# Attention scores as three products of high and low parts in place of one fp32 product

## The chip, the cores and the metric

The kernel runs on one core of one Trainium2 chip. The metric is the device time of one execution in microseconds, the median of the runs shown. Five engines work side by side, each through its own list of instructions in a fixed order: TensorE (PE: matmuls; PEld: the loads of their stationary operand), VectorE (DVE), ScalarE (ACT), GpSimd (POOL) and SyncE (SP, which here only issues transfers).

## The reference

One encoder layer over 1024 rows of 1024 numbers, in fp32. What the change touches is the first part: two attentions over the same normalised rows.

```python
# differential attention, 8 heads, two maps of width 64 each
s = einsum('bqhd,bkhd->bhqk', qq, kk) * scale + bias        # bias: -slope * distance
p = softmax(where(allowed, s, -inf))                        # allowed: key chunk <= query chunk
a = p(map 1) - lam * p(map 2);   o = a @ v                  # then a norm over each head
# chunk attention, 8 heads of width 64: each chunk of 64 sees itself and 8 chunks before it
s = einsum('bcqhd,bckhd->bhcqk', qc, kb) * dh**-0.5 + bias;  o = softmax(s) @ vb
```

Then `h = x + W_out(gates * projections)`, and a retrieval layer (PEER): each row picks 8 x 16 of 16384 experts by two top-16 searches, takes the experts' `u` rows, a gelu, a softmax weight, and sums their `v` rows.

## The kernel before

The rows are 8 blocks of 128. Blocks 0 and 1 form the first group, blocks 2 to 7 the second. The stages, in the order of the program:

- `Dense` (lines 236 to 302) multiplies the normalised rows by `w_in`, tile by tile, and stores q, k, v and gates to DRAM. Its products use three single-pass matmuls of high and low parts: `split` (L124) casts fp32 to the type fp32r on ScalarE (L126: the high part) and subtracts on VectorE (L127: the low part), `mm3` (L129) issues high x high, high x low, low x high.
- `attention` (L304) runs four times: for block 0, for block 1, for blocks 2 and 3 (below: the pair stage), and for blocks 4 to 7 (below: the rest stage). `weave` (L52) alternates its steps with those of other generators: the pair stage with `Dense` of the second group, the rest stage with `merge` and `sel` of blocks 2 and 3.
- In an attention, `kv_load` fetches keys, values and queries of one head from DRAM into tiles with two buffers each. Partitions 0 to 63 of a key tile hold one map (or one of two heads), 64 to 127 the other. `softmax_in` issues the score products (L347) of the two halves, a piece of up to 512 keys at a time; VectorE adds the bias, writes to SBUF and keeps the minimum (L353); ScalarE takes the exponential (L360). A score tile is one of three PSUM buffers. `later` transposes (L203) and multiplies by the values (L372).
- `merge`/`mop` (L478, L849), `sel` (L857: the choice of experts, `top16` at L558 to L563 and `choose`), `gates` (L643) and, at the end, `dense_experts` (L681), which streams all experts for blocks 2 to 5. For blocks 0, 1, 6 and 7 `experts` (L790) gathers the chosen rows: 128 `u` and 128 `v` rows per block and token, each a gather by GpSimd (L804) and one VectorE product over 128x1024 (L810 for `u`, L816 for `v`). These gather products are spread over the whole program: those of blocks 0 and 1 run beside the attentions.

The generators give an order of issue; a scheduler behind them then fixes the order of each engine's list by its own estimate of when operands are ready. So an edit in one place moves instructions of all stages.

Of the kernel before, what the change touches and what calls it, by code (L numbers as in the profile page):

```python
# [7 lines left out]
F32 = mybir.dt.float32  # L8
F32R = mybir.dt.float32r
# [6 lines left out]
P = 128  # L16
# [56 lines left out]
def layer_kernel(ctx, tc, x, w1, w_in, b_gate, lq1, lk1, lq2, lk2, subln, rel,  # L73
# [230 lines left out]
    def attention(wk, LM, gi, blocks, tr, need, put_d, put_c):  # L304
# [4 lines left out]
        t0 = (blocks[0] - GROUPS[gi][0]) * P  # L309

        def kv_load(ksrc, vsrc, qsrc, kb0):
            kt = wk.tile([P, LM], F32, name="kt", tag="kt")
            vt = wk.tile([P, LM // P, P], F32, name="vt", tag="vt")
            qt = wk.tile([P, T], F32, name="qt", tag="qt")
            for g2 in range(gi + 1):
                ob = GROUPS[g2][0]
                s0 = max(kb0, ob)
                e0 = min(blocks[-1] + 1, ob + len(GROUPS[g2]))
                if s0 >= e0:
                    continue  # L320
                nc.sync.dma_start(kt[:, (s0 - kb0) * P:(e0 - kb0) * P], ksrc[g2][:, (s0 - ob) * P:(e0 - ob) * P])
                nc.sync.dma_start(vt[:, s0 - kb0:e0 - kb0, :],
                                  vsrc[g2][(s0 - ob) * P:(e0 - ob) * P, :].rearrange("(n p) f -> p n f", p=P))
            nc.sync.dma_start(qt, qsrc[:, t0:t0 + T])
            return kt, vt, qt

        def sc_tile():
            return psp.tile([P, 512], F32, name="sc", tag="sc", bufs=3)
# [9 lines left out]
        def softmax_in(todo):  # L338


            mns = [None] * len(todo)
            for n in range(len(todo[0][2])):
                os = []
                for q, k, pieces, pt, scale in todo:
                    k0, k1, bias = pieces[n]
                    o = sc_tile()
                    nc.tensor.matmul(o[:, :k1 - k0], q, k[:, k0:k1], start=True, stop=True)  # L347
                    os.append(o)
                for i, (q, k, pieces, pt, scale) in enumerate(todo):
                    k0, k1, bias = pieces[n]  # L350
                    d = k0 - pieces[0][0]
                    mn = sm.tile([P, 1], F32, name="mn", tag="mn", bufs=8)
                    nc.vector.tensor_tensor_reduce(pt[:, d:d + k1 - k0], os[i][:, :k1 - k0], bias, scale,  # L353
                                                   3.0e38 if mns[i] is None else mns[i], OP.add, OP.min, mn)
                    mns[i] = mn
            zs = []
            for i, (q, k, pieces, pt, scale) in enumerate(todo):
                d = pieces[-1][1] - pieces[0][0]
                z = sm.tile([P, 1], F32, name="z", tag="z", bufs=8)
                nc.scalar.activation(pt[:, :d], pt[:, :d], AF.Exp, bias=mns[i], scale=-1.0, accum_out=z)  # L360
                zs.append(z)
            return zs
# [12 lines left out]
        def diff_a(h, i, qb):  # L375
            if i == 0:
                need(h)
                kv[h] = kv_load({g: kd[g][h] for g in kd}, {g: vd[g][h] for g in vd}, qd[gi][h], 0)
            kt, vt, qt = kv[h]
            n = (qb + 1) * P  # L380
            pieces = [(c, min(n, c + 512), dm[:, 896 - P * qb + c:896 - P * qb + min(n, c + 512)])
                      for c in range(0, n, 512)]
            pm = [wk.tile([P, LM], F32, name=f"p{m}", tag="p", bufs=PBUFS) for m in range(2)]
            Z = softmax_in([(qt[rs, i * P:(i + 1) * P], kt[rs], pieces, pt, 2.0 ** -(h + 1))
                            for rs, pt in zip(HALVES, pm)])
            rz1 = sm.tile([P, 1], F32, name="rz1", tag="rz1")
            rz2 = sm.tile([P, 1], F32, name="rz2", tag="rz2")
            f = sm.tile([P, 1], F32, name="f", tag="f")
            nc.vector.reciprocal(rz2, Z[1])
            nc.vector.reciprocal(rz1, Z[0])  # L390
            nc.vector.scalar_tensor_tensor(f, Z[0], nlam, rz2, op0=OP.mult, op1=OP.mult)
            nc.vector.scalar_tensor_tensor(pm[0][:, :n], pm[1][:, :n], f, pm[0][:, :n], op0=OP.mult, op1=OP.add)

            if i % tr == 0:
                ohs[h] = wk.tile([P, tr, P], F32, name="oh", tag="oh")
            oh = ohs[h]

            def later():
                o = pv(pm[0], qb + 1, vt, 0)
                oi = oh[:, i % tr, :]  # L400
                nc.scalar.activation(oi, o[:, :P], AF.Copy, scale=rz1)
                k = h * nb + i
                nc.scalar.activation(scr, oi, AF.Square, accum_out=ssh[:, k:k + 1])
                if i % tr == tr - 1:
                    put_d(h, i + 1 - tr, transposes([oh[:, i2, :] for i2 in range(tr)])[:, :tr * P])
            return later
# [14 lines left out]
        def chunk_a(hp, i, qb):  # L421
            kb0 = max(0, blocks[0] - 4)
            if i == 0:
                need(8 + hp)
                kv[8 + hp] = kv_load({g: kc[g][hp] for g in kc}, {g: vc[g][hp] for g in vc}, qc[gi][hp], kb0)
            if i % tr == 0:
                och[hp] = wk.tile([P, tr, P], F32, name="och", tag="oh")
            oh = och[hp]
            kt, vt, qt = kv[8 + hp]
            k0 = max(0, qb - 4)  # L430
            j0 = (k0 - qb + 4) * P
            off = (k0 - kb0) * P - j0
            pts = [wk.tile([P, LM], F32, name=f"pc{m}", tag="p", bufs=PBUFS) for m in range(2)]
            todo = []
            for m in range(2):
                pieces = []
                if j0 < 384:
                    pieces.append((off + j0, off + 384, far[:, j0:384]))
                c = max(j0, 384)
                pieces.append((off + c, off + 640, nbias[:, 2 * hp + m, c - 384:256]))  # L440
                todo.append((qt[HALVES[m], i * P:(i + 1) * P], kt[HALVES[m]], pieces, pts[m], 1.0))
            rzs = []
            for z in softmax_in(todo):
                rz = sm.tile([P, 1], F32, name="rz", tag="rzc", bufs=8)
                nc.vector.reciprocal(rz, z)
                rzs.append(rz)

            def later():
                for rs, pt, rz in zip(HALVES, pts, rzs):
                    o = pv(pt, qb + 1 - k0, vt, k0 - kb0)  # L450
                    nc.scalar.activation(oh[:, i % tr, rs], o[:, rs], AF.Copy, scale=rz)
                if i % tr == tr - 1:
                    put_c(hp, i + 1 - tr, transposes([oh[:, i2, :] for i2 in range(tr)])[:, :tr * P])
            return later
# [498 lines left out]
```

## Time and profile before

| | us |
|---|---|
| median of 3 runs (lowest, highest) | 3437.65 (3435.08, 3438.16) |
| the profiled execution | 3433.26 |
| its span, first to last instruction | 3431.5 |
| PE busy in the span | 3085.0 (90%) |
| DVE busy | 2700.0 (79%) |
| ACT busy | 1446.3 (42%) |
| POOL busy | 1249.1 (36%) |

The stages lie in the span about so: attention of blocks 0 and 1 from 0 to 300 us, the pair stage from 450 to 960, the rest stage from 1000 to 1460, merges, gates and choices up to 1960, the streamed experts from 2020 to the end. A busy share is an average over stages; what an edit is worth is read from the stage that it is in. PE counts as busy while any matmul is in flight, drain included.

### The profile page before, as it was taken

The numbers are of one execution on the slowest core, as the hardware profiler recorded it, in microseconds if no ns is written. First come the engines' busy times: TensorE is split into PE (matmuls) and PEld (weight loads), VectorE is DVE, ScalarE is ACT, GpSimd is POOL, SyncE is SP. The second block draws the span as 40 slices with busy tenths as digits, with TensorE's granted clock in tenths as the row PEclk, the third lists the DMA queues.
The fourth block names the chain that finished last, engine by engine and source line by source line (L and its number), as shares of the span: only waits on it lengthen the run. The fifth ranks groups of instructions, "written<-read, shape, count | busy, mean of one in ns | idle before, by whom it ended". The sixth has DMA issues, their size and how long they took to land.

```text
span 3431.5 us, 48288 instructions
## 1 busy us (share of the span) xinstructions
PE 3085.0 (90%) x16032; PEld 2551.8 (74%) x16032; DVE 2700.0 (79%) x5848; ACT 1446.3 (42%) x3029; POOL 1249.1 (36%) x1028
## 2 busy tenths in 40 slices
PE   7987699999979886987798359999999999999998
PEld 7986578888857654676677348888888888888886
DVE  4436897777779899987976978889998888999543
ACT  5634433434423544567669523333233333333332
POOL 0000455555544522344000144555555555555000
PEclk9999899999989987998898669999999999999999
DMA  7675999999999975898544499999999999999531
GB/s 240 219 244 189 374 333 348 333 352 334 326 340 351 324 236 186 281 360 331 203 162 157 145 343 319 346 350 339 347 345 345 346 342 344 346 340 349 166 123 49
DMA packets 406122, 987.13 MB, mean 288 GB/s; under 512 B 43184, under 2 KB 188400, under 8 KB 403696
## 3 DMA queue, kind: packets, MB, share of 16 engines
q0 software_dynamic: 147456, 536.94, 44.1%
q1 hardware_dynamic: 258416, 447.11, 37.4%
q8 instruction: 126, 2.06, 0.2%
q14 instruction: 124, 1.02, 0.1%
HBM read 905.72 MB, written 78.15 MB: 287 GB/s over the span
## 4 chain that ended last, share of the span: by engine, by line
PE 71%; issue 12%; DVE 7%; DMA 7%; ACT 2%; POOL 1%; SPq 0%; DVEq 0%; POOLq 0%; ACTq 0%
PE ph L134 20%; PE mm L134 16%; PE acc L710 15%; PE acc L717 5%; PE mm L490 5%; PE sc L347 3%; PE pv L372 3%; PE tr L203 2%; DMA ge<-in_u_dram,ei 2%; DVE junk L810 1%; DVE p L353 1%; POOL ge L804 1%; DMA rb<-rst 1%; DMA ge<-in_v_dram,ei 1%; DVE acc L816 1%
## 5 line engine op out<-in xcount | busy, mean ns | idle before, releaser
L804 POOL DMA_INDIRECT ge<-in_u_dram,ei x512 | 619.1, 1209 | 1249.0 <-DVE junk L810 396.4
L804 POOL DMA_INDIRECT ge<-in_v_dram,ei x512 | 629.8, 1230 | 683.2 <-DVE acc L816 462.0
L816 DVE SCALAR_TENSOR_TENSOR acc<-ge,a,acc 128x1024 f32<-128x1024 f32 x512 | 655.1, 1280 | 26.2 <-DMA ge<-in_v_dram,ei 20.1
L810 DVE SCALAR_TENSOR_TENSOR junk<-ge,xs 128x1024 bf16<-128x1024 f32 x512 | 624.7, 1220 | 53.7 <-DMA ge<-in_u_dram,ei 45.7
L127 DVE TENSOR_TENSOR wl<-wr,wh 128x1024 fp32r<-128x1024 f32 x232 | 283.6, 1223 | 233.1 <-ACT wh L126 107.5
L126 ACT CAST wh<-wr 128x1024 fp32r<-128x1024 f32 x232 | 243.7, 1051 | 406.5 <-PE ph L134 267.1
L134 PE MATMUL ph<-x2h,wh 128*128 128x512 f32 x1024 | 400.3, 391 | 11.8 <-ACT wh L126 10.4
L134 PE MATMUL ph<-x2l,wh 128*128 128x512 f32 x1024 | 399.9, 390 | 0.0
L134 PE MATMUL mm<-xh,wh 128*128 128x256 f32 (+1 forms) x1248 | 372.0, 325 | 0.7 <-ACT st L286 0.5
L134 PE MATMUL mm<-xl,wh 128*128 128x256 f32 (+1 forms) x1248 | 366.8, 321 | 1.4 <-DVE xl L232 1.3
L134 PEld LDWEIGHTS mm<-xh,wh 128*128 128x128 f32 x1248 | 236.9, 190 | 24.8 <-ACT st L286 2.3
L134 PE MATMUL ph<-x2h,wl 128*128 128x512 f32 x1024 | 253.1, 389 | 0.0
L134 PEld LDWEIGHTS mm<-xl,wh 128*128 128x128 f32 x1248 | 236.4, 190 | 21.5 <-DVE xl L232 2.1
L126 ACT CAST vh<-vr 128x512 fp32r<-128x512 f32 x256 | 140.4, 619 | 264.8 <-PE acc L717 243.4
L134 PE MATMUL mm<-xh,wl 128*128 128x256 f32 (+1 forms) x1248 | 234.4, 323 | 0.0
L134 PEld LDWEIGHTS ph<-x2h,wh 128*128 128x128 f32 x1024 | 193.2, 189 | 52.9 <-ACT wh L126 10.8
L134 PEld LDWEIGHTS ph<-x2l,wh 128*128 128x128 f32 x1024 | 193.2, 189 | 40.2
L134 PEld LDWEIGHTS ph<-x2h,wl 128*128 128x128 f32 x1024 | 192.3, 188 | 40.0
L347 PE MATMUL sc<-kt,qt 64*128 64x256 f32 (+3 forms) x608 | 202.1, 533 | 17.8 <-DVE mn L353 10.2
L710 PE MATMUL acc<-vh,ah 128*128 128x512 f32 x768 | 198.3, 389 | 0.0
L126 ACT CAST ah<-ge 128x512 fp32r<-128x512 f32 x128 | 79.7, 622 | 281.4 <-DVE ge L757 266.3
L134 PEld LDWEIGHTS mm<-xh,wl 128*128 128x128 f32 x1248 | 184.7, 189 | 16.8
(199 smaller groups left out, 5741.6 us busy)
## 6 DMA issues: line engine op xcount, KB each, us to landing
vr<-in_v_dram SPq DMA_DIRECT2D x128, 512.0 KB
wr<-in_ut_dram SPq DMA_DIRECT2D x128, 512.0 KB
wr<-in_w_in_dram SPq DMA_DIRECT2D x104, 512.0 KB
gdr<-gst SPq DMA_DIRECT2D x16, 2048.0 KB
gj<-gdr SPq DMA_DIRECT2D x512, 64.0 KB
wr<-in_w_bd_dram SPq DMA_DIRECT2D x40, 512.0 KB
wr<-in_w_out_dram SPq DMA_DIRECT2D x40, 512.0 KB
wr<-in_wq_dram SPq DMA_DIRECT2D x40, 512.0 KB
```

The source lines that it names most:

```text
L126: nc.scalar.copy(hi, raw)
L127: nc.vector.tensor_sub(lo, raw, hi.bitcast(F32))
L134: nc.tensor.matmul(o, w[a][:, k, :], xx[b][:, k, :], start=(i == 0), stop=(i == last))
L203: nc.tensor.transpose(o[:, i * P:(i + 1) * P], s, ident)
L347: nc.tensor.matmul(o[:, :k1 - k0], q, k[:, k0:k1], start=True, stop=True)
L372: nc.tensor.matmul(o[:, :P], aT[:, j - c, :], vt[:, v0 + j, :], start=(j == 0), stop=(j == n - 1))
L490: nc.tensor.matmul(o, w[:, k, :], xx[:, k, :], start=(k == 0), stop=(k == K - 1))
L710: nc.tensor.matmul(acc[i][hf], a[x][:, i * P:(i + 1) * P], b[y][:, hf * 512:hf * 512 + 512], **kw)
L717: nc.tensor.matmul(o, aa[:, 3 * P:4 * P], bb[:, cs], start=(n == 0), stop=(n == len(todo) - 1))
L804: nc.gpsimd.indirect_dma_start(out=t, out_offset=None, in_=src, in_offset=bass.IndirectOffsetOnAxis(ap=ei[:, k:k + 1], axis=0))
L810: nc.vector.scalar_tensor_tensor(junk, t, 1.0, xs, op0=OP.mult, op1=OP.mult, accum_out=hid[:, k:k + 1])
L816: nc.vector.scalar_tensor_tensor(acc, t, a[:, k:k + 1], acc, op0=OP.mult, op1=OP.add)
```

## The change

Keys and queries are loaded into tiles of type fp32r and split there: ScalarE casts the loaded tile into a new tile (`kth`, `qth`: the high part), VectorE subtracts in place (`ktl`, `qtl` then hold the low part). Each score product, one fp32 matmul before, becomes three fp32r matmuls that accumulate in PSUM: high x high, high query x low key, low query x high key. The loop is turned round so that the two halves alternate within each of the three.

```diff
         def kv_load(ksrc, vsrc, qsrc, kb0):
-            kt = wk.tile([P, LM], F32, name="kt", tag="kt")
+            ktl = wk.tile([P, LM], F32R, name="ktl", tag="ktl")
+            kt = ktl.bitcast(F32)
             vt = wk.tile([P, LM // P, P], F32, name="vt", tag="vt")
-            qt = wk.tile([P, T], F32, name="qt", tag="qt")
+            qtl = wk.tile([P, T], F32R, name="qtl", tag="qtl")
+            qt = qtl.bitcast(F32)
...
             nc.sync.dma_start(qt, qsrc[:, t0:t0 + T])
-            return kt, vt, qt
+            n = (blocks[-1] + 1 - kb0) * P
+            two = []
+            for lo, m, name in ((ktl, n, "kt"), (qtl, T, "qt")):
+                hi = wk.tile(list(lo.shape), F32R, name=name + "h", tag=name + "h")
+                split(lo[:, :m].bitcast(F32), hi[:, :m], lo[:, :m])
+                two.append((hi, lo))
+            return two[0], vt, two[1]
...
-            for n in range(len(todo[0][2])):
-                os = []
-                for q, k, pieces, pt, scale in todo:
-                    k0, k1, bias = pieces[n]
-                    o = sc_tile()
-                    nc.tensor.matmul(o[:, :k1 - k0], q, k[:, k0:k1], start=True, stop=True)
-                    os.append(o)
+            for n in range(len(todo[0][4])):
+                os = [sc_tile() for _ in todo]
+                for j, (a, b) in enumerate(((0, 0), (0, 1), (1, 0))):
+                    for o, (rs, qs, q, k, pieces, pt, scale) in zip(os, todo):
+                        k0, k1, bias = pieces[n]
+                        nc.tensor.matmul(o[:, :k1 - k0], q[a][rs, qs], k[b][rs, k0:k1], start=(j == 0), stop=(j == 2))
```

Line numbers behind the first hunk are 7 or 8 higher in the kernel after: L355 there are the score products, L360 the reductions (L353 before), L817 and L823 the gather products (L810, L816).

The first place is VectorE's list at the start of the rest stage (`mT`, `g`: the merge; `p`: scores with bias; `junk`: a gather product). Before:

```order
L511 TENSOR_TENSOR mT<-g_9528 128x256
L508 SCALAR_TENSOR_TENSOR g_9609<-g_9609,mm 128x256
L353 ISA p_9442,mn<-sc,dm 128x512
L353 ISA mn 128x1
L353 ISA p_9443,mn<-sc,dm 128x512
```

After:

```order
L518 TENSOR_TENSOR mT<-g_9990 128x256
L515 SCALAR_TENSOR_TENSOR g_10079<-g_10079,mm 128x256
L127 TENSOR_TENSOR ktl<-ktl,kth 128x1024
L817 SCALAR_TENSOR_TENSOR junk,hid<-ge,xs_29040 128x1024
L127 TENSOR_TENSOR qtl<-qtl,qth 128x512
L127 TENSOR_TENSOR ktl<-ktl,kth 128x1024
L360 ISA p_9888,mn<-sc,dm 128x512
L360 ISA mn 128x1
L360 ISA p_9889,mn<-sc,dm 128x512
```

Three subtractions and a gather product now stand ahead of the first reduction; the second `ktl` is that of the next head.

The second place is TensorE's list in the rest stage, among the merge's products (`mm<-mT,wr`). Before:

```order
L203 MATMUL tr<-ident,p_10265 128x128 x4
L347 MATMUL sc<-kt,qt 128x512 x2
L490 MATMUL mm<-mT,wr 128x256 x2
L203 MATMUL tr<-ident,p_10265 128x128 x4
L490 MATMUL mm<-mT,wr 128x256 x4
L347 MATMUL sc<-kt,qt 128x384
```

After:

```order
L203 MATMUL tr<-ident,p_10463 128x128 x8
L355 MATMUL sc<-kth,qth 128x512 x2
L355 MATMUL sc<-ktl,qth 128x512 x2
L355 MATMUL sc<-kth,qtl 128x512 x2
L355 MATMUL sc<-kth,qth 128x256
L355 MATMUL sc<-ktl,qth 128x256
L355 MATMUL sc<-kth,qtl 128x256
L497 MATMUL mm<-mT,wr 128x256 x8
```

Rows with x2 are the two halves in turn. The three rows without it are all of one half; this form makes up most of the rest stage, since a product waits for a free score tile.

The third place is VectorE's list just ahead of the choice for block 4 (`cand`), behind the last gate tile of blocks 2 and 3; `acc<-ge,a,acc` is a gather product of a `v` row. Before:

```order
L561 MATCH_REPLACE qs<-vv,qs 128x128 x2
L787 SCALAR_TENSOR_TENSOR acc<-acc,nr,wfb 128x1024
L561 MATCH_REPLACE qs<-vv,qs 128x128 x2
L562 MAX vv<-qs 128x8 x2
L559 MAX vv<-qs 128x8 x4
```

After:

```order
L823 SCALAR_TENSOR_TENSOR acc<-ge,a,acc 128x1024
L568 MATCH_REPLACE qs<-vv,qs 128x128 x4
L566 MAX vv<-qs 128x8 x4
L823 SCALAR_TENSOR_TENSOR acc<-ge,a,acc 128x1024
L569 MAX vv<-qs 128x8 x4
L567 MAX_INDEX iu<-vv,qs 128x8 x4
L823 SCALAR_TENSOR_TENSOR acc<-ge,a,acc 128x1024
```

Before, the gather products of block 1 are through here and its rows go out (L787, the final norm); after, they still stand between the searches. Counted over the list: 444 of the 512 gather products of blocks 0 and 1 stood ahead of the last score reduction, now 433; 509 ahead of the last gate tile of blocks 2 and 3, now 501; all 512 ahead of the gate tiles of blocks 4 and 5, as before.

## Rows read from the trace of the kernel before

**Rows 1.** Busy us (instructions) by stretch: length, PE, PEld, DVE, ACT, POOL; clock, DMA.

```profile
0.00:300.00 300.00, 264.86 (x2036) 245.64 (x2037) 134.18 (x411) 160.12 (x414) 0.20 (x4) 0.98 0.72 228
450.00:960.00 510.00, 508.61 (x3002) 428.89 (x3002) 396.15 (x645) 197.58 (x408) 277.31 (x225) 1.00 0.95 340
...
1000.00:1140.00 140.00, 140.00 (x684) 97.53 (x682) 129.20 (x316) 56.70 (x137) 65.39 (x59) 1.00 0.94 338
1200.00:1360.00 160.00, 124.48 (x517) 81.92 (x516) 158.62 (x640) 66.24 (x160) 42.10 (x43) 0.80 0.65 208
1360.00:1460.00 100.00, 97.60 (x567) 68.39 (x565) 89.77 (x220) 59.27 (x153) 38.85 (x39) 0.99 0.83 276
1460.00:1640.00 180.00, 144.27 (x829) 127.73 (x830) 146.93 (x275) 127.51 (x299) 72.17 (x58) 0.90 0.91 340
1640.00:1700.00 60.00, 42.71 (x268) 37.26 (x266) 60.00 (x268) 42.37 (x98) 5.56 (x5) 0.89 0.63 226
...
2020.00:3431.00 1411.00, 1394.96 (x6143) 1154.14 (x6141) 1139.81 (x1494) 446.19 (x687) 614.73 (x480) 0.99 0.85 302
```

**Rows 2.** Chain of waits by line, 1000 to 1140 us: share of the stretch.

```profile
by line: PE mm L490 46.9%; PE sc L347 28.6%; PE pv L372 15.4%; PE tr L203 9.5%
```

**Rows 3.** Chain of waits in order of time, 960 to 1000 us: start, length, what.

```profile
978.91 11.69 DMA kt<-kd
990.65 0.69 DVE p L353
```

**Rows 4.** Score products (L347) alone, rest stage: length, PE busy, PEld busy (records).

```profile
960.00:1460.00 500.00, 146.67 (x384) 52.08 (x384) 0.89 0.83 283
```

**Rows 5.** Timeline of PE, pair stage: start us, us, instruction, operand shapes, records merged.

```profile
526.25 1.12 PE L347 MATMUL sc<-kt,qt 64*128 64x512 f32 x2
527.30 0.94 PE L372 MATMUL pv<-vt,aT 128*128 128x128 f32 x6
...
571.63 1.13 PE L347 MATMUL sc<-kt,qt 64*128 64x512 f32 x4
572.69 0.50 PE L134 MATMUL mm<-xh,wh 128*128 128x512 f32 x1
```

**Rows 6.** Timeline of PE in other stages: fp32 products, then single-pass ones.

```profile
1472.93 3.62 PE L490 MATMUL mm<-on,wr 128*128 128x256 f32 x16
1476.38 1.28 PE L372 MATMUL pv<-vt,aT 128*128 128x128 f32 x10
...
2056.24 1.52 PE L710 MATMUL acc<-vh,ah 128*128 128x512 f32 x6
2057.60 1.52 PE L710 MATMUL acc<-vl,ah 128*128 128x512 f32 x6
```

**Rows 7.** Groups by line and shape: xcount, busy us, mean ns, idle before.

```profile
L127 DVE TENSOR_TENSOR wl<-wr,wh 128x1024 fp32r<-128x1024 f32 x232 | 283.6, 1223 | 233.1 <-ACT wh L126 107.5 <-PE ph L134 71.7 <-PE mm L134 31.8
L127 DVE TENSOR_TENSOR vl<-vr,vh 128x512 fp32r<-128x512 f32 x256 | 164.3, 687 | 0.7 <-ACT vh L126 0.6
L511 DVE TENSOR_TENSOR mT<-g 128x256 f32<-128x256 f32 x24 | 9.9, 416 | 0.0
L232 DVE SCALAR_TENSOR_TENSOR xl<-tr,w1c,xh 128x128 fp32r<-128x128 f32 x64 | 20.8, 344 | 7.1 <-ACT xh L231 6.5 <-issue 0.2
L126 ACT CAST wh<-wr 128x1024 fp32r<-128x1024 f32 x232 | 243.7, 1051 | 406.5 <-PE ph L134 267.1 <-PE mm L134 74.0 <-issue 34.2
L816 DVE SCALAR_TENSOR_TENSOR acc<-ge,a,acc 128x1024 f32<-128x1024 f32 x512 | 655.1, 1280 | 26.2 <-DMA ge<-in_v_dram,ei 20.1 <-DVE o L663 0.3
```

**Rows 8.** Gathers on POOL (L804) by stretch: length, POOL busy (gathers).

```profile
985.00:1460.00 475.00, 179.97 (x169) 0.90 0.81 278
...
1640.00:1700.00 60.00, 5.56 (x5) 0.89 0.63 226
1700.00:1958.00 258.00, 0.00 (x0) 0.84 0.41 145
```

**Rows 9.** Who waited for whom, 1600 to 1720 us: total us, times, longest.

```profile
ACT pf L587 <- DVE ci L563: 19.5, 1, 19.5
```

More of the change, by code (lines that the diff above doesn't have):

```diff
@@ L341, in softmax_in @@
             mns = [None] * len(todo)
-            for n in range(len(todo[0][2])):
-                os = []
-                for q, k, pieces, pt, scale in todo:
-                    k0, k1, bias = pieces[n]
-                    o = sc_tile()
-                    nc.tensor.matmul(o[:, :k1 - k0], q, k[:, k0:k1], start=True, stop=True)
-                    os.append(o)
-                for i, (q, k, pieces, pt, scale) in enumerate(todo):
+            for n in range(len(todo[0][4])):
[4 more added lines that the diff above has]
+                        nc.tensor.matmul(o[:, :k1 - k0], q[a][rs, qs], k[b][rs, k0:k1], start=(j == 0), stop=(j == 2))
+                for i, (rs, qs, q, k, pieces, pt, scale) in enumerate(todo):
                     k0, k1, bias = pieces[n]
@@ L356, in softmax_in @@
             zs = []
-            for i, (q, k, pieces, pt, scale) in enumerate(todo):
+            for i, (rs, qs, q, k, pieces, pt, scale) in enumerate(todo):
                 d = pieces[-1][1] - pieces[0][0]
@@ L383, in diff_a @@
             pm = [wk.tile([P, LM], F32, name=f"p{m}", tag="p", bufs=PBUFS) for m in range(2)]
-            Z = softmax_in([(qt[rs, i * P:(i + 1) * P], kt[rs], pieces, pt, 2.0 ** -(h + 1))
+            Z = softmax_in([(rs, slice(i * P, (i + 1) * P), qt, kt, pieces, pt, 2.0 ** -(h + 1))
                             for rs, pt in zip(HALVES, pm)])
@@ L440, in chunk_a @@
                 pieces.append((off + c, off + 640, nbias[:, 2 * hp + m, c - 384:256]))
-                todo.append((qt[HALVES[m], i * P:(i + 1) * P], kt[HALVES[m]], pieces, pts[m], 1.0))
+                todo.append((HALVES[m], slice(i * P, (i + 1) * P), qt, kt, pieces, pts[m], 1.0))
             rzs = []
```

## The prediction

> **What bounds the kernel now.** I read the stretches first [rows 1], then in each the chain of waits and the waits by pair. From 2020 us on TensorE is busy 1395.0 of 1411 us, with products that the change leaves alone; it moves the end only by the moment at which that stage begins. So the question is how long the front takes, up to 2020 us, and what stands last in each of its stretches. In the first 300 us TensorE is busy for 264.9 and VectorE for 134.2. In the pair stage (450 to 960) TensorE is full, 508.6 of 510, with VectorE at 396.2: TensorE decides. In the rest stage the two take turns. From 1000 to 1140 the chain runs through TensorE alone, 28.6% of it score products [rows 2]; but VectorE is busy for 129.2 of these 140 us. From 1200 to 1360 VectorE has 158.6 of 160 and TensorE waits. From 1360 to 1460 it is 97.6 (TensorE) against 89.8 (VectorE). From 1640 to 1700 VectorE is busy for all 60.0 us [rows 1], in the searches for blocks 4 and 5, and ScalarE waits 19.5 us for one of their results [rows 9]. Gathers explain why VectorE is so full: they run until just before 1700 us and then stop [rows 8], since the choices for blocks 6 and 7 don't exist yet.
>
> **The change, part by part.** *Score products on TensorE.* One product of 512 keys holds TensorE from 526.25 to 527.30, 1.05 us; the two halves issued together take 571.63 to 572.69, 1.06 us [rows 5]. So the second half costs nothing beside the first. The stream: a 256-wide fp32 record takes 3.45/16 = 0.216 us, a 512-wide product is two records of twice that, 0.86 us, which leaves 0.19 us of tail that every run of score products pays before other matmuls go on. A single-pass 512-wide product takes 1.36/6 = 0.227 us [rows 6]; three make 0.68. So a pair goes from 1.06 to about 0.87 us, a gain of 18%, if the halves overlap as they do now.
>
> I counted the runs over the two orders, each with the time of its longer half. Pair stage: 34 runs with 24.5 us of stream become 41 with 18.9 us; a run costs 0.19 us of tail and about 0.1 on the way in, so -5.6 + 7 x 0.3 = **-4 us**, on the engine that decides there, and for that I take it whole (bounds -6 and 0). Rest stage: 127 runs with 89.6 us become 121. Most now hold three products of one half and then three of the other, which no row shows. Bounds: full overlap, 65 us; start in program order, where the second half's first product begins with the first half's third, 80 us. Of the gain of 10 to 24 us some half lies in the 240 us in which TensorE decides: 5 to 12 us, of which I take the middle, 8, for want of a row. The trace has the score products at 146.7 us there, waits in the drain included [rows 4], so nothing larger hides in them.
>
> The Trainium skill (TensorE: Matmul & The Clock Gate, Part 3: Packing small matmuls) says that matmuls start and end strictly in program order, and only weight loads are pulled ahead. The pairs above agree with overlap of row halves but cannot show this rule, as their halves alternate. By it the 80 us hold, the gain there is 5 and not 8, and the sum below would be 3 us higher.
>
> *Splits.* 96 casts and 96 subtractions. VectorE per tile: 1.223 us at 1024 columns, 0.687 at 512, 0.416 at 256, 0.344 at 128 [rows 7]. Block 0: 24 x 0.344 = 8 us; block 1: 12 x (0.416 + 0.344) = 9; pair stage: 12 x (0.687 + 0.416) = 13; rest stage: 12 x (1.223 + 0.687) = 23. The first three lie under a TensorE that decides, VectorE having 166 and 114 us free there: nothing, apart from runs of score products that are broken up (35 become 48 for blocks 0 and 1: 13 x 0.3 = 4 us, of which I take **+2**, bounds 0 and +5; were that cover gone it would be 30). ScalarE pays about as much (1.051 us at 1024) and has the room everywhere. The order puts a head's splits a head ahead of their use, so that only the first head of the rest stage shows them.
>
> *Start of the rest stage.* The chain waits for the key transfer from 978.91 to 990.6, and the first reduction follows at once [rows 3]. Now a cast, two key subtractions and a query one (1.05 + 1.22 + 0.69 + 1.22 = 4.2 us, with the gather product between them 5.5) stand ahead of it. Part of it fits under the transfers still under way: **+2 us** (0 to +5.5).
>
> *Rest stage on VectorE.* 21 more us of subtractions (23 less the first head's). The order takes out 11 gather products (444 ahead of the last reduction become 433), 11 x 1.28 = 14 us [rows 7]. Net +7 us. In the stretches where TensorE decided, VectorE had 21 us free of 240; there the stage shrinks by 8 and VectorE still has room. In the 220 us between, where VectorE decides or shares, it grows by 5. **-3 us** (-12 to +9).
>
> *The gather products come back.* They must all be done before the gates of blocks 4 and 5, as before. 3 of the 11 land among the gates of blocks 2 and 3 (VectorE 146.9 of 180 us), where I take half, 2 us; 8 land behind them, among the searches where VectorE has no idle time: 8 x 1.28 = 10 us. ScalarE's casts of the choice stand behind those searches, and gates and choices behind the casts. Together I take **+11 us** (0 if the freed earlier time is passed on, +14 if all count).
>
> Sum: 2 - 4 + 2 - 3 + 11 = +8 us. On the profiled execution, 3433.3 + 8 = 3441.3; the median of the runs lies 4.4 above that execution, so 3446.
>
> In a sentence: TensorE gains where it decides, a little; VectorE, which is full from 1000 to 1720 us, gets 23 us more, and its gather work only moves back into a stretch that is fuller.
>
> **Rivals.** *Faster: TensorE decides more than I think.* Gathers give way in the rest stage and fit into idle time later; then -6 in the pair stage, -12 in the rest stage, +2 at the beginning, nothing else: -16, so 3422. For it: the chain of 1000 to 1140 [rows 2], and VectorE's 33 idle us from 1460 to 1640. Against it: 60.0 of 60 us behind.
>
> *No change.* Gains and costs cancel: +2 - 4 + 1 - 6 + 7 = 0, so 3438. It needs half of the 11 gather products to find idle time between 1460 and 1700 us, where VectorE has 33 us of it, all ahead of 1640.
>
> *Slower by much: each head waits for its split.* If the key tile comes free so late that the split stands on the path at each head, 11 heads pay a cast (1.05), two subtractions (1.91) and a gather product ahead (1.28): 4.2 x 11 = 47 on top of the other terms, about 3493. It decides when the load of the next head lands after the last reduction of the one before. Against it: two buffers, and an order with a head's lead.
>
> *The halves don't overlap.* Three single-pass products on 64 rows may not run beside the other half's. Then a pair is 6 x 0.227 + 0.19 = 1.55 us, not 1.06: the pair stage streams 28.6 us (+4 in place of -6) and the rest stage 98 (half of +8 felt, 4, in place of -8): 3446 + 10 + 12 = 3468.
>
> **Chances.** Forecast 0.44 (its own range 3437 to 3459), faster 0.20, no change 0.22, waits at each head 0.06, no overlap 0.08. The range for 8 in 10: 3424 to 3464; it leaves out the waits at each head, half of the rival on the fast side and no overlap. A measurement tells about 0.2% from no change, 6.9 us: below 3430.8 is faster, above 3444.5 slower. Slower: 0.32 of the forecast, 0.06, 0.08 and 0.02 of no change, 0.48. Same: 0.12 and 0.18, 0.30. Faster: 0.20 and 0.02, 0.22.
>
> **What the profile after would show.** Two score products of 512 keys that alternate: about 0.87 us to the next matmul; 1.5 or more means no overlap. The pair stage about 4 us shorter with TensorE full. The first reduction of the rest stage about 2 us later behind the key transfer. VectorE in the rest stage at 95% or more with some 158 gathers where there are 169 [rows 8], and some 18 gather products, in place of 10, on a full VectorE just ahead of the choice for block 4. The streamed experts begin about 8 us later and take as long as before. I am wrong if they begin earlier, if VectorE has idle time between 1640 and 1700 us, or if TensorE waits for `ktl` at the heads of the rest stage.

## The result and the profile after

| | before | after |
|---|---|---|
| median of 6 runs each (lowest, highest), us | 3439.99 (3435.08, 3443.53) | 3463.33 (3459.34, 3474.53) |
| profiled execution, us | 3433.26 | 3465.05 |
| granted clock over the span | 0.944 | 0.935 |

The ratio is 1.0074 (95% interval 1.0055 to 1.0092): the medians lie 23.3 us apart, the profiled executions 31.8. The prediction had the sign (3446, 3424 to 3464) and a third of the size; the measured median lies 0.7 us inside the upper end of its range.

Busy time by stretch after, in the columns of [rows 1], each stretch moved by what the work in it had moved:

```profile
0.00:300.00 300.00, 262.06 (x2010) 245.14 (x2010) 136.83 (x403) 161.80 (x439) 0.20 (x4) 0.96 0.70 222
470.00:980.00 510.00, 505.50 (x3049) 434.02 (x3049) 401.51 (x638) 205.67 (x430) 272.20 (x222) 1.00 0.95 337
...
1660.00:1732.00 72.00, 44.98 (x277) 39.17 (x273) 71.73 (x289) 40.58 (x92) 15.13 (x15) 0.84 0.74 255
2051.00:3463.00 1412.00, 1396.05 (x6144) 1155.38 (x6144) 1140.56 (x1494) 446.11 (x687) 610.39 (x480) 0.99 0.85 301
```

Little differs in busy time. The stretch before the choice of block 4, with VectorE full, is 72 us and no longer 60; the streamed experts take 1412 us, as before, and begin 31.9 us later. The columns do not show where these come from. For that, landmarks serve: the first matmul of a `Dense` tile, the last score reduction, the first matmul of the streamed experts. The table has the length of each stretch before and, for each kernel, what its profiled execution is longer (start of one landmark less start of the one ahead). Each line is one execution. That of the kernel before is 6.7 us under the median of its six, so the other lines come out some us long in all. The streamed experts, behind the last column, take as long as before within 1.3 us, but for e1 (+3.9).

```
                          1st Dense   2nd Dense,  to its   to its    last     tail to   gather products
                          to tile 52  to tile 5   tile 15  last one  reduct.  experts   in the tail
                          (0-192)     (-474)      (-573)   (-951)    (-1459)  (-2019)
before, us                  191.8        281.8        99.1     378.4    507.6    560.3      68
after                       +11.1         +9.1        -0.6      -1.6     +1.4    +12.5      79
e1  blocks 0,1 as before     -0.3         +0.1        +9.1      -0.6     -0.5    +19.1      82
e2  only blocks 0,1          +8.2         +6.1        +2.6      -1.9     -1.1     +1.5      69
e3  casts 0,1 on GpSimd      +0.6         -3.0        +0.1      -0.7    +14.4    +20.0      80
e4  splits alone             +8.6        +11.4        +1.5      -0.9    +22.7     +1.2      68
e5  rest as before           +8.7        +11.2        +0.4      -1.6     +4.5     +0.3      67
e6  products alone           +1.6         -5.4        +0.2      -1.2     +6.6    +16.7      80
e7  halves written apart     +9.5         +2.6        +0.7      +1.9     +7.5    +16.6      77
e8  split where made        +16.4        +16.8        +9.3      +2.1    -11.4    +45.4     102
e9  casts alone             +11.5         +7.0        +6.8      +1.2     +5.3     -2.4      65
e10 subtractions alone       +0.2        +17.0        -0.8      -0.1    +16.7     +1.7      64
e11 only rest                -0.4         -2.9        +1.6       0.0     -0.7    +18.8      82
e12 only pair                -0.5         +0.5        +9.2      -0.5     +2.4     +3.6      68
e13 only rest, 14 fewer      -0.2          0.0         0.0       0.0     +1.9     +1.8      68
e14 GpSimd casts, 0 to 3     +1.5         -1.6        +5.2      +0.2     +7.3     +7.8      69
e15 GpSimd casts, pair       -1.0         +0.7        +6.5      -0.5     +9.4     +1.7      66
e16 before, queries first    +1.0         +0.6        -0.5       0.0     -5.0     +5.8      72
```

The line of the changed kernel: 20.2 us are lost by 474 us, 2.2 come back in the pair stage, the rest stage adds 1.4, the tail behind it 12.5. The first loss is seen where the second `Dense` tile of a head is under way. First ScalarE, then TensorE (start us, us, instruction; in brackets the idle time before it and what ended it):

```profile
64.16 0.19 ACT L410 ACTIVATION_READ_ACCUMULATOR scr<-oh 128x1 f32 x1
69.84 0.30 ACT L126 CAST kth<-ktl 128x128 fp32r<-128x128 f32 x1 [5.49 <-DMA ktl<-kd]
70.04 1.04 ACT L126 CAST wh<-wr 128x1024 fp32r<-128x1024 f32 x1
70.99 0.36 ACT L292 COPY st<-mm 128x256 f32<-128x256 f32 x1
```

```profile
67.48 1.12 PE L134 MATMUL mm<-xh,wl 128*128 128x256 f32 x8
71.40 0.69 PE L203 MATMUL tr<-ident,st 128*128 128x128 f32 x2 [2.80 <-ACT st L292]
...
73.34 0.41 PE L134 MATMUL mm<-xl,wh 128*128 128x256 f32 x1
...
78.19 0.28 PE L134 MATMUL mm<-xl,wh 128*128 128x256 f32 x1
```

`kth` is the high part of a head whose keys `Dense` has only just stored; ScalarE stands 5.49 us for their transfer, and behind the cast stand the cast of the next weights and the eviction of the tile before (`st`, L292), for which TensorE waits 2.80 us. Then a record of 256 columns takes 0.41 us and not 0.28, until 78 us: the clock has fallen. Columns as in [rows 1]:

```profile
60.00:69.00 9.00, 8.24 (x66) 7.76 (x64) 3.48 (x6) 4.23 (x12) 0.00 (x0) 1.00 0.68 208
69.00:72.00 3.00, 0.60 (x2) 0.29 (x2) 1.18 (x2) 1.78 (x4) 0.00 (x0) 0.75 0.25 90
72.00:78.00 6.00, 6.00 (x33) 5.86 (x33) 3.18 (x11) 3.88 (x10) 0.00 (x0) 0.56 0.69 223
```

A granted clock of 0.56 is nearly all at the lower level, 1.2 of 2.4 GHz. Tile 13 began 2.8 us late, tile 15 begins 8.2 us late. Such waits add up, from 0 to 215 us (who waits for whom: total us, times, longest); the keys and queries of the other attention add 6.6 us:

```profile
ACT kth L126 <- DMA ktl<-kd: 27.0, 10, 5.5
ACT qth L126 <- DMA qtl<-qd: 9.3, 9, 1.8
```

Before, ScalarE waits for no key or query transfer at all; TensorE, whose score products alone read those tiles, waits 0.5 us for one.

### The profile page after: what moved, and what is told of

Its sections match the earlier page's. It is cut to its first block, busy times and chain, and to the rows that moved or that the text cites. A ratio compares the mean times of both kernels' runs of the same rounds, so it can differ in the third digit from the quotient of the medians.

```text
span 3463.2 us, 49213 instructions
## 1 busy us (share of the span) xinstructions
PE 3083.9 (89%) x16336; PEld 2600.8 (75%) x16336; DVE 2743.0 (79%) x5944; ACT 1479.1 (43%) x3125; POOL 1252.0 (36%) x1028
## 4 chain that ended last, share of the span: by engine, by line
PE 60%; issue 10%; DVE 8%; DMA 5%; ACT 2%; POOL 1%; SPq 0%; DVEq 0%; ACTq 0%; POOLq 0%
PE ph L134 20%; PE acc L717 15%; PE mm L134 11%; PE acc L724 5%; PE mm L497 3%; PE pv L379 2%; PE sc L355 2%; PE tr L203 2%; DVE junk L817 1%; DVE acc L823 1%; DMA ge<-in_u_dram,ei 1%; DVE p L360 1%; DMA rb<-rst 1%; DMA ktl<-kd 1%; POOL ge L811 1%
## 5 line engine op out<-in xcount | busy, mean ns | idle before, releaser
L823 DVE SCALAR_TENSOR_TENSOR acc<-ge,a,acc 128x1024 f32<-128x1024 f32 x512 | 654.8, 1279 | 23.1 <-DMA ge<-in_v_dram,ei 17.2
L817 DVE SCALAR_TENSOR_TENSOR junk<-ge,xs 128x1024 bf16<-128x1024 f32 x512 | 624.1, 1219 | 46.2 <-DMA ge<-in_u_dram,ei 41.3
L717 PE MATMUL acc<-vl,ah 128*128 128x512 f32 x768 | 195.0, 389 | 0.0
```

Of the source, the lines that this page charges most:

```text
L717: nc.tensor.matmul(acc[i][hf], a[x][:, i * P:(i + 1) * P], b[y][:, hf * 512:hf * 512 + 512], **kw)
L817: nc.vector.scalar_tensor_tensor(junk, t, 1.0, xs, op0=OP.mult, op1=OP.mult, accum_out=hid[:, k:k + 1])
L823: nc.vector.scalar_tensor_tensor(acc, t, a[:, k:k + 1], acc, op0=OP.mult, op1=OP.add)
```

## The experiments

Each is a version of the changed kernel unless said otherwise. "Measured" gives the median, the ratio to the kernel before and its interval.

### Blocks 0 and 1 undone, and alone (e1, e2)

The products become `terms`, one or three; e1 leaves blocks 0 and 1 as before (`gi == 0`), e2 the other stages (`gi == 1`):

```
+            if gi == 0:
+                return (kt,), vt, (qt,)
...
+                terms = ((0, 0),) if gi == 0 else ((0, 0), (0, 1), (1, 0))
+                for j, (a, b) in enumerate(terms):
```

> Blocks 0 and 1 (everything up to about 450 us) take their scores as before: no split, one fp32 product. The later stages stay as in the changed kernel. Theory A (the first 200 us lose 11 to 12 us because the splits' casts stand at the head of ScalarE's list and wait for the key and query transfers, in front of Dense's weight casts; the start of the second Dense loses 9 more because it meets the queue of VectorE at another phase): the first merge starts at 199 us again and the whole comes to 3443 to 3452. Rival B (the loss lies in the rest stage and behind it, where VectorE is full, and earlier delays are only passed through): the whole stays at 3459 or more.

> The reverse: only blocks 0 and 1 take three products on split tiles, the pair stage and the rest stage are as in the kernel before. Theory A: first merge 11 to 12 us later than before, second Dense 18 to 20 later, end 10 to 20 us over before, 3450 to 3460. Rival B (cost is in the rest stage): 3440 to 3444.

Measured: e1 3461.36, 1.0060 (1.0043 to 1.0077); e2 3452.74, 1.0035 (1.0021 to 1.0049). Theory A is right on the place and wrong on the sum: by its time e1 is what rival B forecast, e2 what theory A did. In e1 the first 474 us are as before, to 0.3 us, and nothing is won at the end: 9.1 us are lost at the start of the pair stage and 19.1 in the tail, where 82 gather products stand. e2 loses the front (+14.3 by tile 5) and nothing behind. So the losses are several and do not add: the one at the pair stage does not show in the changed kernel, whose front is late.

### The cast on GpSimd in blocks 0 and 1 (e3)

```
-                split(lo[:, :m].bitcast(F32), hi[:, :m], lo[:, :m])
+                if gi == 0:
+                    nc.gpsimd.tensor_copy(hi[:, :m], lo[:, :m].bitcast(F32))
+                    nc.vector.tensor_sub(lo[:, :m], lo[:, :m].bitcast(F32), hi[:, :m].bitcast(F32))
```

> The changed kernel, but in blocks 0 and 1 GpSimd makes the high part in place of ScalarE; GpSimd is idle in this stage. Subtractions, tiles and products stay. Theory A (ScalarE's list is held up by the wait for the transfers): the first merge starts at 199 to 203 us and the whole comes to 3445 to 3455. Rival C (runs of score products that are broken up, or the 24 small splits on VectorE, cost the 11 us): the first merge still starts at 208 us or later and the whole is 3460 or more.

Measured: 3463.09, 1.0065 (1.0046 to 1.0085). The first half came as theory A has it: the first `Dense` takes 0.6 us longer and not 11.1, and the second `Dense` is 2.4 us earlier than before. The waits have gone to an engine that nobody needs there (0 to 200 us):

```profile
POOL kth L332 <- DMA ktl<-kd: 90.6, 9, 35.7
POOL qth L332 <- DMA qtl<-qd: 23.8, 10, 3.8
```

So the first loss is the place of the cast, not the subtractions and not broken runs of score products (rival C). The end missed its expectation: +14.4 in the rest stage, +20.0 in the tail. Its rest stage has the work of the changed kernel's (VectorE is busy for 461.7 us, in the changed kernel for 461.4), which lost 1.4; why it loses 14.4 here is open.

### Splits alone, casts alone, subtractions alone, products alone (e4, e9, e10, e6)

e4 writes both parts into `hi`, which nothing reads, and takes one fp32 product on the loaded tile; e9 keeps only the cast, e10 only a subtraction of the same shape. e6 has no split and takes three products of the loaded tiles themselves (the scores are three times too large).

```
e4   +  split(lo[:, :m].bitcast(F32), hi[:, :m], hi[:, :m])
e9   +  nc.scalar.copy(hi[:, :m], lo[:, :m].bitcast(F32))
e10  +  nc.vector.tensor_sub(hi[:, :m], lo[:, :m].bitcast(F32), lo[:, :m].bitcast(F32))
e6   -  split(lo[:, :m].bitcast(F32), hi[:, :m], lo[:, :m])
     +  two.append((lo, lo))
```

> All splits are made, into a tile that no product reads; the scores are one fp32 product on the loaded tile, as before. So VectorE and ScalarE pay all, TensorE gains nothing and no product waits for a split. Theory A (TensorE's gain is 2 to 4 us in all, the waits on ScalarE stay): 3462 to 3470. Rival D (waits of score products for their split are what costs, the engines' extra work is hidden): 3440 to 3448.

> The kernel before plus ScalarE's 96 casts of the loaded tiles into a tile that nothing reads; no subtraction, one fp32 product on the loaded tile. Theory A (a cast at the head of ScalarE's list waits for its transfer and holds up Dense's weight casts and evictions): the second Dense starts 8 to 20 us later than before, nothing is added behind it, the whole is 3448 to 3460. Rival V (the front is as long as VectorE's work in it plus a fixed idle time, so only VectorE's work counts): 3436 to 3443.

> The kernel before plus the 96 subtractions on VectorE (the loaded tile minus itself, into a tile that nothing reads); no cast, one fp32 product. Rival V: the 52 us of VectorE's work come out at 0.7 to 1 each, 3475 to 3492. The prediction's view (30 of the 52 lie under a TensorE that decides, the other 22 in the rest stage count): 3455 to 3464. Theory A says of this only that the front up to 300 us stays as before.

> Three single-pass products on the loaded tiles as they are, no split at all (each product takes the same two tiles, so the scores are three times too large). TensorE has all of the change, ScalarE and VectorE none. Theory A: TensorE saves 2 to 6 us in the stages where it decides and nothing is lost: 3434 to 3440. Rival F (TensorE itself loses, by more and shorter runs of score products): 3445 or more.

Measured: e4 3473.75, 1.0091 (1.0074 to 1.0109); e9 3468.56, 1.0085 (1.0066 to 1.0105); e10 3468.28, 1.0078 (1.0060 to 1.0095); e6 3452.55, 1.0035 (1.0021 to 1.0049).

Casts alone cost 11.5 us in the first `Dense`, where the whole change costs 11.1, with the same waits (e9, 0 to 200 us):

```profile
ACT kth L331 <- DMA ktl<-kd: 28.9, 9, 5.3
ACT qth L331 <- DMA qtl<-qd: 12.5, 8, 3.1
```

ScalarE's busy time, 160.12 of 300 us before [rows 1], said nothing of this. Rival V falls with it: no work of VectorE was added. e9 came out above its range, since the pair stage and the rest stage lost 13.3 more. Subtractions alone leave the first `Dense` as it was and cost 17.0 behind it. There VectorE, busy with `merge` and the searches, now waits at the head of its list for the same transfers (200 to 490 us):

```profile
DVE kth L331 <- DMA ktl<-kd: 8.3, 5, 2.4
DVE kth L331 <- DMA ktl<-kc: 4.5, 4, 2.8
DVE qth L331 <- DMA qtl<-qc: 3.0, 2, 2.0
```

These 15.8 us come near the loss, but the sum of such waits is no price: in the first 200 us VectorE waits 41.2 us for these transfers, and the first `Dense` loses 0.2. In the rest stage VectorE is busy for 470.3 us, 15.5 more than before, and the stage is 16.7 longer. The whole, 3468.28, lies between the two ranges expected. e4 pays both (+20.0 by tile 5, +22.7 in the rest stage) and came out above its range.

e6 is the surprise: TensorE's side of the change, with nothing else, makes the kernel slower. The front is 3.8 us shorter by tile 5, the rest stage 6.6 longer, the tail 16.7 longer. Its expectation named another cause (rival F, broken runs), and the pair stage, 1.0 us shorter on a full TensorE, speaks against that there. The last column names the tail's part: 80 gather products, without a single subtraction that could have pushed them there. The 6.6 us of the rest stage, where VectorE is busy for 442.0 us and not 454.8, stay open.

### The rest stage undone, and alone (e5, e11); 14 gathers left out (e13)

The edit of e1 with `LM == S` (e5), with `LM < S` (e11). e13 is e11 with

```
-        for k in range(K):
-            t = gather(v, k)
+        for k in range(K - 14 if b == 1 else K):
+            t = gather(v, k)
```

> The rest stage (blocks 4 to 7) takes its scores as before, without splits; blocks 0 and 1 and the pair stage stay as in the changed kernel. Theory A (of the 23 us about 12 come from gather products that the rest stage's splits push behind 1460 us, the rest from the first 480 us): the second Dense starts 18 to 20 us later than before, the stretch from the last score reduction to the choice of block 4 is as long as before, and the whole comes to 3448 to 3455. Rival E (the early delay is made up later, all the loss is in the rest stage): 3440 to 3444.

> Only the rest stage takes three products on split tiles (blocks 4 to 7); blocks 0 to 3 as before. Theory A with the list (10 to 14 gather products stand behind the last score reduction more than before, 1.3 us each, and the stage itself gains nothing): up to 960 us as before, 77 to 82 gather products behind the last reduction where there are 68, the whole 3452 to 3460. Rival V (23 us of VectorE's work at full price): 3463. Rival H (the loss of the rest stage is carried in from the front): 3440.

> As the run that changes the rest stage alone (3449.9 us), but the last 14 gathers of block 1 and their products are left out, so that 68 of them stand behind the last score reduction in VectorE's list, as in the kernel before, and not 82. If the loss behind the last reduction is the gather products that stand there: 14 x 1.3 us less, 3429 to 3434, and from the last reduction to the streamed experts 560 us as before. If something else lengthens that stretch: 3446 to 3452.

Measured: e5 3455.60, 1.0044 (1.0027 to 1.0062); e11 3449.88, 1.0028 (1.0017 to 1.0038); e13 3438.40, 1.0001 (0.9993 to 1.0010). e5 brings the tail back to 560.7 with 67 gather products and leaves the front where it was (+19.9). e11 is as before up to the last score reduction (-2.4 there) and then loses 18.8. The tail in columns as in [rows 1], before, after, e11 and e13:

```profile
1458.70:2019.00 560.30, 385.03 (x2170) 336.80 (x2170) 456.93 (x1503) 360.21 (x821) 115.20 (x96) 0.83 0.65 235
1478.10:2050.90 572.80, 387.06 (x2170) 336.96 (x2168) 469.88 (x1517) 358.96 (x819) 125.20 (x107) 0.83 0.67 240
1456.30:2035.40 579.10, 387.50 (x2170) 337.57 (x2169) 473.67 (x1522) 358.77 (x819) 128.27 (x110) 0.82 0.67 241
1460.40:2022.50 562.10, 387.02 (x2170) 335.66 (x2168) 457.12 (x1506) 359.23 (x819) 110.78 (x96) 0.83 0.64 235
```

The products of `v` rows among them, VectorE alone, e11 and e13 (length, busy, count, clock, DMA share, GB/s):

```profile
1456.30:2035.40 579.10, 104.31 (x82) 0.82 0.67 241
1460.40:2022.50 562.10, 86.97 (x68) 0.83 0.64 235
```

With 14 products taken out the tail shrinks from 579.1 to 562.1, 1.2 us for each, and the median by 11.5, 0.8 for each. That is the cause, shown by taking it away; and in all four lines VectorE is idle for 103 to 105 us, so the tail is as long as VectorE's work in it makes it. The times were not all as expected: e5 lies 0.6 us above its range, e11 2.1 below, e13 between its two, though its tail is as forecast. Over all lines of the table the count goes by the score products of the rest stage: with one fp32 product the tail holds 64 to 72, with three single-pass ones 77 to 82 (e8: 102; e13: 82 less the 14), split or not.

### The pair stage alone (e12), with casts on GpSimd (e15), and all but the rest (e14)

The edit of e1 with `LM != 4 * P` (e12); the same with every split's cast on GpSimd (e15); those casts with `LM == S` undone (e14).

> Only the pair stage (blocks 2 and 3) takes three products on split tiles. The prediction's term (TensorE decides there, 4 us less, the splits hidden): 3433 to 3438. Rival V (13 us of VectorE's work at 0.7 to 1): 3447 to 3453.

> Only the pair stage is changed, as in the run at 3442.7, and its casts are on GpSimd; 66 gather products behind the last reduction. If ScalarE's wait for the second head's keys (520 to 535 us) is what cost 9 us there: pair stage 1 to 4 us shorter than before, the whole 3431 to 3437. If the wait only moves to GpSimd and its gathers, or the late split is late on any engine: 3441 to 3447.

> Three products on split tiles in blocks 0 to 3 with all casts on GpSimd, the rest stage as before; 69 gather products behind the last reduction. If the waits on ScalarE were the loss of the front and TensorE's gain is what is left: second Dense 2 to 3 us earlier than before, end of the pair stage 3 to 6 earlier, the whole 3432 to 3438. If the casts on GpSimd hold up its gathers in the pair stage: 3443 to 3455.

Measured: e12 3442.66, 1.0008 (0.9998 to 1.0019); e15 3456.10, 1.0056 (1.0041 to 1.0072), its profiled execution 6.2 us under that; e14 3444.37, 1.0016 (1.0006 to 1.0026). The time of e12 lies in neither of its ranges and is not clear of the kernel before. In its profiled execution the stage that should have gained 4 us loses 9.2 at its start and gains 0.5 behind. The timeline of e12 there (start us, us, instruction; in brackets the idle time before it and what ended it):

```profile
521.22 0.44 PE L358 MATMUL sc<-kth,qth 64*128 64x384 f32 x2
...
522.32 0.62 ACT L126 CAST kth<-ktl 128x512 fp32r<-128x512 f32 x1 [5.67 <-DMA ktl<-kd]
522.97 0.69 DVE L127 TENSOR_TENSOR ktl<-ktl,kth 128x512 fp32r<-128x512 f32 x1 [3.88 <-ACT kth L126]
523.58 0.42 DVE L127 TENSOR_TENSOR qtl<-qtl,qth 128x256 fp32r<-128x256 f32 x1
523.91 1.22 DVE L820 SCALAR_TENSOR_TENSOR junk<-ge,xs 128x1024 bf16<-128x1024 f32 x1
525.06 0.55 DVE L363 CUSTOM_DVE_ANT_0 p<-sc,dm 128x384 f32<-128x384 f32 x1
525.67 0.49 PE L358 MATMUL sc<-kth,qth 64*128 64x512 f32 x1 [2.31 <-DVE mn L363]
```

The score products of the first head begin at 521.22, so its own split is done (its casts started at 512.22 and 516.25). What is late is the split of the second head: its keys land only now, and VectorE's list has it ahead of the first head's reductions. VectorE stands 3.88 us for it, the first reduction starts at 525.06 (before, at 520.36), and TensorE waits 2.31 us for a score tile and 3.07 soon after. This is the loss of the front over again, in another list. Moving the cast does not help here: in e15, with the cast on GpSimd, the same transfer ends at 520.53, the subtraction of the second head still stands ahead of the reductions, and 6.5 us are lost. That is what the second of its expectations says of the place; its time is above both ranges, with 9.4 us lost in the rest stage that no run explains. In the changed kernel, 20 us late by then, the place is passed without loss (-0.6).

e14 has nothing left of the loss of the front (-0.1 by tile 5). Its time is that of the second expectation, but held-up gathers were not shown: 5.2 us are lost at the start of the pair stage, 7.3 in the rest stage, 7.8 in the tail with 69 gather products, and the last two are open. Its profiled execution is the longest of its twelve, 8.3 us over their median.

### Halves written apart (e7), split where made (e8), a neutral edit (e16)

```
e7   -  for j, (a, b) in enumerate(((0, 0), (0, 1), (1, 0))):
     -      for o, (rs, qs, q, k, pieces, pt, scale) in zip(os, todo):
     +  for o, (rs, qs, q, k, pieces, pt, scale) in zip(os, todo):
     +      for j, (a, b) in enumerate(((0, 0), (0, 1), (1, 0))):
e8   +  nc.scalar.activation(s.bitcast(F32R), o, AF.Copy, scale=scale)
     +  nc.vector.scalar_tensor_tensor(sl, o, scale, s, op0=OP.mult, op1=OP.subtract)
     +  nc.sync.dma_start(dst[0][:, c:c + n * P], s)
     +  nc.sync.dma_start(dst[1][:, c:c + n * P], sl.bitcast(F32))
e16  (kernel before)
     +  nc.sync.dma_start(qt, qsrc[:, t0:t0 + T])
        for g2 in range(gi + 1):
```

> The changed kernel with the three products of one map written ahead of the three of the other. If a product of one row half starts only when the one ahead in the list has started, the second half begins with the third product of the first and a pair of 512 keys takes 5 x 0.23 + 0.2 = 1.35 us to the next matmul in place of 0.90: pair stage 5 to 10 us longer, the whole 3468 to 3478. If the halves overlap whatever their order: pair again 0.90 us and the whole within 4 us of 3463.

> The parts are made once, where Dense evicts a key or query tile (ScalarE writes the high part in its eviction, VectorE the low part, 48 subtractions of 256 to 512 columns); both go to memory and are loaded as two tiles. No split stands behind a load. Theory A: no head of ScalarE's list waits for a key transfer, the rest stage's VectorE is freed of 23 us; the whole is 3430 to 3445. Rival G (12 x 0.75 MB more to load in the rest stage, whose queues are at 0.9: 9 MB at 0.34 MB per us is 27 us, felt in gathers or heads): 3455 or more.

> The kernel before with one edit that changes no work: a head's query tile is loaded ahead of its keys and values. It shows how far the time moves when only the lists come out otherwise. 72 gather products stand behind the last reduction, where there are 68: by 1.3 us each 3440 to 3446; without such an effect 3436 to 3440.

Measured: e7 3473.45, 1.0107 (1.0086 to 1.0127); e8 3509.27, 1.0188 (1.0164 to 1.0213); e16 3439.90, 1.0010 (0.9996 to 1.0023). e7 lies in the range of its first expectation, but its time is no proof of it: the scheduler alternates the halves again in most of its list (52 pairs, 54 in the changed kernel), and such pairs still take 0.90 us. Against the changed kernel its front is 8.1 us shorter, its pair stage 4.8 longer, the rest stage 6.1 and the tail 4.1 longer. The rows that do answer its question stand below, under the pair stage. e8 is far from theory A; its time is that of rival G, but the loss is not where G has it: with the parts made in `Dense` 42.5 us are lost by its tile 15, by what waits is open, and 102 gather products end in the tail. Only the rest stage gained (-11.4), with 22 gather products fewer in it. e16 has the same work as before and other lists: -5.0 in the rest stage, +5.8 in the tail with 72 gather products, and no difference in all. Single stretches of the table are thus known to some 5 us. The tails, at 1.2 us for each product above or below 68, come out between 1 us shorter and 7 us longer than their count says (e14 and e10 are the furthest).

No version beat the kernel before.

## Why the prediction was wrong

**The step that failed** is the first term: that the splits up to 300 us "lie under a TensorE that decides" and cost nothing there, apart from **+2** for broken runs, and that "ScalarE pays about as much (1.051 us at 1024) and has the room everywhere". It was +11.1 in the first `Dense` and +9.1 from there to 474 us, for which there was no term. Room was counted as idle time. What counted was the place in the list: a cast that waits for a transfer holds up the evictions behind it, e9 shows the cost without anything else, e3 takes it away by moving the cast. The prediction looked for lateness only where score products read the tiles. The Trainium skill (PSUM — Partial Sum Buffer, Engine vs sequencer instructions) says that the queues of ScalarE, VectorE and GpSimd are strictly first in, first out; the rows at 69.84 us agree, and this was the rule to weigh against the change. The 9.1 go with the casts too: e9, casts alone, loses 7.0 there, and e3, which keeps the subtractions behind a cast on GpSimd, is 3.0 us shorter. Which waits make them up is open, since e10, without a cast, loses 17.0 at the same place.

**Pair stage, -4.** -2.2 from tile 5 on. The working was nearly right: a pair of 512 goes from 1.06 [rows 5] to 0.90 us, where 0.87 was forecast, with both halves side by side (a pair of the rest stage):

```profile
1056.09 0.51 PE L355 MATMUL sc<-kth,qth 64*128 64x512 f32 x2
...
1056.66 0.40 PE L355 MATMUL sc<-kth,qtl 64*128 64x512 f32 x2
1056.99 2.00 PE L497 MATMUL mm<-ocx,wr 128*128 128x256 f32 x8
```

So the rival that the halves don't overlap falls. The trace of e7 also has what the rest stage's bounds turned on, two triples one behind the other:

```profile
1146.38 0.49 PE L355 MATMUL sc<-kth,qth 64*128 64x512 f32 x1
...
1146.94 0.39 PE L355 MATMUL sc<-kth,qtl 64*128 64x512 f32 x1
1147.04 0.50 PE L355 MATMUL sc<-kth,qth 64*128 64x512 f32 x1
```

The second triple begins 0.10 us after the third product of the first, and its last product starts at 1147.61, 1.23 us behind the first of all; in the alternating pair that is 0.57. At 72 such places in the traces of twelve kernels the second triple never starts ahead of the first's third product, at four it starts within 0.02 us of it. So the traces bear out the start in program order; by the prediction's own working the gain to take for the rest stage was then 5 and not 8 us.

That the term came out near its size is partly luck. The rival that heads wait for their split was weighed at 0.06, for all heads; e1, e12 and e15 show 6 to 9 us lost at one head when the front is on time, and not by its own split but by that of the next head, which "a head ahead of their use" puts in front of its reductions. A late front hid this.

**Start of the rest stage, +2.** Right in size. The first reduction comes 41.8 us behind the last `Dense` tile, where it came 39.6, 2.2 us behind a key transfer:

```profile
997.97 10.73 DMA ktl<-kd
...
1008.72 1.05 ACT kth L126
...
1010.94 0.68 DVE p L360
```

The transfer, though, is that of the next head, after and in [rows 3] as well: the first head's score products start at 1007.54, and started at 988.47. Before, the reduction reads nothing of that tile; its own score products end at 990.55 and the transfer at 990.60, too close together for the trace to tell which released it. After, the cast and the subtraction of the next head's keys stand ahead of the reduction, as in e12.

**Rest stage, -3.** -0.8 without its start. VectorE has 6.5 us more work in a stage that is 1.4 us longer, before and after (columns of [rows 1]):

```profile
951.10:1458.70 507.60, 439.86 (x2118) 304.78 (x2116) 454.83 (x1344) 223.16 (x543) 196.98 (x184) 0.89 0.83 286
969.10:1478.10 509.00, 426.02 (x2312) 333.79 (x2311) 461.36 (x1358) 241.15 (x570) 197.70 (x174) 0.86 0.81 275
```

In some runs the stage follows VectorE's work: e10 has 15.5 us more and +16.7, e11 the subtractions less 14 gather products and -0.7. In e3 and e6 it does not, so this is argued and not shown. The 8 us taken for stretches in which TensorE decides did not show; the stage ran at a granted clock of 0.86 where it had 0.89.

**Gather products, +11.** 79 in the tail where there were 68, as counted, and 12.5 us. Most of the signs forecast for it hold: 160 gathers from 1005 to 1478 us against 169 [rows 8], 18 products ahead of the choice of block 4 against 10, VectorE busy for 71.73 of 72 us. VectorE in the rest stage did not reach 95%: it has 440.4 of 473.0 us from 1005 us on, 93%. The splits are not the reason: e6 moves 12 products without any. What moves them is argued, not shown: by the scheduler's estimate three single-pass products leave a shorter rest stage, into which fewer gather products fit. On the chip the stage is no shorter (e6: longer by 6.6), and they come back where VectorE is full.

By terms: the front failed by 18 us, the others together by 6; with the +8 forecast that makes the 32 measured in the profiled executions. The medians are 23 apart, so some 8 of the 32 belong to these two executions and to no term.

## What to carry to other kernels

An engine with much idle time is no cover for an instruction that waits: ask what stands behind it in the same list, and whether its input is still under way. Work put in a list early, for the next head, holds up this head when its input is late. Where a scheduler fills a full engine's list with background work, count how much of that work each version leaves behind the stage; here each item left cost about 1.2 us, whatever the stage itself had gained. And test a change of three parts part by part: here the gainful part lost alone, and undoing one place moved its loss to the next.

## Not expected of the hardware

A wait of TensorE of 2.80 us (69 to 72 us, busy for 0.60 of 3.00) was followed by 6 us at a granted clock of 0.56. In e12 waits of 2.31 and 3.07 us, ended at 525.67 and 532.15, go with 16 us at 0.57:

```profile
520.00:526.00 6.00, 3.69 (x18) 2.32 (x17) 3.03 (x7) 1.37 (x3) 0.88 (x2) 1.00 0.99 391
526.00:542.00 16.00, 12.93 (x58) 10.96 (x57) 15.85 (x44) 9.07 (x26) 7.84 (x8) 0.57 0.84 262
```

By an estimate from these rows the lower clock cost 6.00 x 0.44 = 2.6 and 12.93 x 0.43 = 5.6 us, about as much again as the waits themselves (2.8 and 5.4).

One triple of 512 keys on 64 rows takes 0.90 us to the next matmul (541.70 to 542.60 us after), and so does a pair of alternating triples on the two halves.
